# Three Strassen-like sets of projections in a hybrid decoder layer: the gates' set first, the group's attention behind the last set, and both halves of a weight's cast issued inside one job

## The chip, the cores and the metric

The kernel runs on one core of a Trainium2 chip. The metric is the device time of one execution in microseconds (us), lower is better. The kernel before was timed three times: 1045.32, 1046.86 and 1047.52 us, median 1046.86.

## What is computed

One layer of a decoder trunk on 512 tokens of width 1024, all in float32. `u` is the normed input. One wide projection gives queries, keys and values of three attention groups, the input of a pooling branch, the inputs of a state-space branch (`z`, `xbc`, `dt`) and three gates.

```python
u = rmsnorm(x, ln1_g[i])
proj = u @ w_in[i]
q, k, v, pool_in, z, xbc, dt_raw, gate_pre = jnp.split(proj, split_idx, axis=-1)
y_a = dilated_attention_mixer(q, k, v, rel_bias) @ w_a[i]
y_b = pool_mixer(pool_in, pool_w[i], pool_scale[i]) @ w_b[i]
y_c = ssd_mixer(z, xbc, dt_raw, ...) @ w_c[i]
gates = jax.nn.sigmoid(gate_pre + b_gate[i]).reshape(b, s, N_BRANCH, D_MODEL)
merged = gates[:, :, 0] * y_a + gates[:, :, 1] * y_b + gates[:, :, 2] * y_c
x = x + merged @ w_o[i]
x = x + conv_ffn(rmsnorm(x, ln2_g[i]), ...)
return rmsnorm(x, final_g)
```

## The kernel before

**Products.** A float32 product is made of three passes on TensorE (`mm3`, L234): weight and activation are each split into a rounded part and a remainder, and high x high, high x low and low x high are summed in PSUM. The activations `uh` and `ul` are split once. A weight is split for each job: a DMA brings `raw` (L183, SP's queue), ACT rounds it into `wh` (`cast`, L195), DVE subtracts to get `wl` (`low`, L215). `wh` has three buffers, `wl` and `raw` two.

**Jobs and their order.** `program()` yields the jobs in a list written by hand; between them stand `Call`s, which run other code at that place. Every engine works through its own instructions in the order in which this Python emits them. Ahead of job n, `prepare` emits `low` of job n+1, `cast` of job n+2 in two halves, and the DMA of job n+3. The two halves of a cast are not emitted at once: they wait in the list `second`. `flush()` emits what waits there, and the first half puts the second one into the list. `flush()` is called by every `step()` and, until the list is empty, ahead of each job. `step()` also takes the next item from `waiting` (attention heads, state-space chunks) and moves the running ones on by one stage, so these small pieces lie between jobs.

**The three sets.** Twelve blocks of 128 columns (queries and keys of attention group 1, and six of the eight blocks of gate 1; the other two are ordinary jobs) are computed in three sets. A set takes two blocks as its left side and two as its right side and replaces eight products of half size by seven, the jobs "one" to "seven": each 24 matmuls of 128x256 with sums of the activations (`sah`, `sbh`) and of the weights. The weights of "two" and "three" come by DMA as `raw`; the others are made in the set's tile `W`, by DVE (`plus`, L349) and by adding DMAs from POOL (L370). Behind its matmuls a job's `use` takes the PSUM bank: ACT copies it (L731), then the sinks of the blocks finish it. A query or key sink is one DVE or ACT operation (L678, L681, L689). A gate sink adds on DVE (L1221, L1229), takes the sigmoid on ACT (L1215) and multiplies into `MG` on DVE (the tile `yo`, L1218); in job "seven" it does this for one block after the other.

Before, the sets were: set 0 with queries and keys 0 and 1; set 1 with query and key 2 and gates 0 and 1; set 2 with gates 2 to 5. The sets overlap in a fixed list; written as (set, job), the last nine are (2, one), (1, seven), (2, five), (1, four), (2, three), (2, two), (2, six), (2, seven), (2, four), with a spare `xbc` job (a whole block, `pa`, 24 matmuls of 128x512) ahead of (2, seven) and of (2, four). The first nine are (0, one), (0, five), (0, two), (0, three), (0, six), (1, one), (0, seven), (1, five), (0, four). Behind (1, four) stood `attend(1)`, which puts six head items and the statistics of group 1 into `waiting`. An item: scores on TensorE (`ps`, L799), bias and maximum on DVE (L813, L817), four exponentials with sums on ACT (L820), transposes on TensorE (`pt`, L827), a copy, and for each pair the output product (`po`, L840). Behind the sets come `BC(0, 8)`, eight blocks of `xbc` in four jobs with ordinary `pa` chunks, then `ssd_start` (twelve Silu on ACT, L1144) and the queries and keys of group 2 (`pqk`).

## Time and profile before

| | us |
|---|---|
| median of three runs | 1046.86 |
| the profiled execution | 1044.88 |
| its span on the core | 1043.1 |
| TensorE (PE) busy | 1025.3 |
| DVE busy | 699.1 |
| ACT busy | 490.1 |

The profiled execution is 1.78 us longer than its span, and 1.98 us under the median. Rows of the timeline give start, duration, engine, line, operation with output and inputs, shape, and in brackets how long the engine stood idle ahead of it and what ended that. A row may merge several instructions (x4). Matmuls are pipelined, so starts are to be compared, not ends. PEclk is the clock granted to TensorE, 1.00 being full speed. The chain of waits is followed back from the last instruction.

### The profile page before, as it was taken

What the parts mean: (1) busy time and instruction counts of PE and PEld (TensorE: products, weight loads), DVE (VectorE), ACT (ScalarE), POOL (GpSimd) and SP (SyncE); (2) the same over time, 40 slices, a digit from 0 to 9 for tenths busy, and PEclk for the clock granted to TensorE, in tenths of its full rate; (3) what the DMA queues carried; (4) which work ended last, traced back from release to release, by engine and by line L of the source; (5) the groups of instructions that cost most, each with busy time, mean ns of one, the idle gap of its engine ahead of it and who ended that gap; (6) DMA issues with size and microseconds to landing.
All of it is one profiled execution on the core that took longest, in us unless ns stands there. A gap on an engine that the chain in (4) does not pass through costs nothing.

```text
span 1043.1 us, 13694 instructions
## 1 busy us (share of the span) xinstructions
PE 1025.3 (98%) x5420; PEld 870.1 (83%) x5420; DVE 699.1 (67%) x938; ACT 490.1 (47%) x815; POOL 161.7 (15%) x135
## 2 busy tenths in 40 slices
PE   9999999999988999999999999999999999999997
PEld 9998878899977878888888888898888888888885
DVE  5553566777757658767667755767677776766775
ACT  5432544445557454565565333545445344453342
POOL 1770000001100003310134500001110000111120
PEclk9999999999998999999999999999999999999999
DMA  8344312156532236453244535443223324323142
GB/s 285 116 128 137 116 46 74 33 135 147 119 104 91 82 101 162 94 155 77 81 132 140 178 100 210 165 143 112 91 81 122 119 73 172 121 81 122 61 141 81
DMA packets 121919, 123.16 MB, mean 118 GB/s; under 512 B 5603, under 2 KB 104230, under 8 KB 121855
## 3 DMA queue, kind: packets, MB, share of 16 engines
q1 hardware_dynamic: 118543, 119.07, 36.2%
q0 software_dynamic: 2720, 2.36, 1.7%
q8 instruction: 42, 0.69, 0.3%
q10 hardware_dynamic: 592, 0.86, 0.2%
q14 instruction: 22, 0.18, 0.1%
HBM read 118.48 MB, written 2.22 MB: 116 GB/s over the span
## 4 chain that ended last, share of the span: by engine, by line
PE 93%; ACT 3%; DVE 2%; DMA 1%; issue 0%; ACTq 0%; DVEq 0%
PE pa L234 31%; PE pu L234 22%; PE p L234 15%; PE pb L234 8%; PE pqk L234 6%; PE pa L1696 2%; PE pu L1481 1%; PE ppw L234 1%; PE ps L799 1%; PE po L840 1%; PE pt L827 1%; PE py L1125 1%; DVE wl L215 1%; ACT sb L820 1%; DMA xin<-in_x_dram 1%; ACT wh L195 1%
## 5 line engine op out<-in xcount | busy, mean ns | idle before, releaser
L215 DVE TENSOR_TENSOR wl<-raw,wh 128x2048 fp32r<-128x2048 f32 (+3 forms) x94 | 208.8, 2223 | 57.3 <-ACT wh L195 50.1
L195 ACT CAST wh<-raw 128x1024 fp32r<-128x1024 f32 (+3 forms) x186 | 180.8, 994 | 44.5 <-DVE raw L339 26.4
L1342 DVE SCALAR_TENSOR_TENSOR hc<-pu,fcol,hc 128x510 f32<-128x510 f32 x88 | 65.8, 748 | 61.1 <-ACT hc L1339 59.5
L234 PE MATMUL pa<-uh,wh 128*128 128x512 f32 x336 | 87.8, 404 | 3.5 <-ACT wh L195 3.5
L234 PE MATMUL pu<-uh,wl 128*128 128x512 f32 (+1 forms) x352 | 83.7, 380 | 0.0
L234 PE MATMUL pu<-uh,wh 128*128 128x512 f32 (+1 forms) x352 | 83.5, 379 | 0.0
L234 PE MATMUL pu<-ul,wh 128*128 128x512 f32 (+1 forms) x352 | 83.5, 379 | 0.0
L234 PE MATMUL pa<-uh,wl 128*128 128x512 f32 x336 | 83.1, 389 | 0.4 <-DVE wl L215 0.4
L234 PE MATMUL pa<-ul,wh 128*128 128x512 f32 x336 | 83.1, 389 | 0.0
L234 PEld LDWEIGHTS pa<-uh,wh 128*128 128x128 f32 x336 | 62.2, 191 | 16.9 <-ACT wh L195 4.1
L234 PEld LDWEIGHTS pu<-uh,wl 128*128 128x128 f32 x352 | 64.1, 188 | 12.8 <-DVE wl L215 0.3
L234 PEld LDWEIGHTS pu<-ul,wh 128*128 128x128 f32 x352 | 64.2, 188 | 12.5
L234 PEld LDWEIGHTS pa<-uh,wl 128*128 128x128 f32 x336 | 63.0, 188 | 13.8 <-DVE wl L215 0.8
L234 PEld LDWEIGHTS pu<-uh,wh 128*128 128x128 f32 x352 | 64.1, 188 | 12.4
L234 PEld LDWEIGHTS pa<-ul,wh 128*128 128x128 f32 x336 | 63.1, 188 | 13.3
L1347 POOL TENSOR_TENSOR hc<-hc 128x512 f32<-128x512 f32 x22 | 30.4, 1382 | 278.9 <-DVE hc L1342 243.9
L1339 ACT ACTIVATE hc<-pu,fcol,fcol 128x512 f32<-128x512 f32 x40 | 31.2, 780 | 81.2 <-PE pu L234 80.9
L215 DVE TENSOR_TENSOR wl<-w,wh 128x1024 fp32r<-128x1024 f32 (+2 forms) x25 | 38.5, 1541 | 10.6 <-ACT wh L195 10.6
L820 ACT ACTIVATE sb<-sb,both 128x128 f32<-128x128 f32 (+1 forms) x72 | 30.1, 419 | 27.7 <-DVE both L817 17.6
L370 POOL DMA_DIRECT2D w<-in_w_in_dram x10 | 12.3, 1230 | 194.4 <-DVE w L349 164.8
L195 ACT CAST wh<-w 128x512 fp32r<-128x512 f32 (+2 forms) x50 | 35.2, 746 | 15.0 <-DVE w L349 9.7
L1344 ACT ACTIVATE hc<-hc 128x512 f32<-128x512 f32 x22 | 13.9, 632 | 42.7 <-DVE hc L1342 42.7
(382 smaller groups left out, 1955.7 us busy)
## 6 DMA issues: line engine op xcount, KB each, us to landing
raw<-in_ffn_w_up_dram SPq DMA_DIRECT2D x22, 1024.0 KB
raw<-in_w_in_dram SPq DMA_DIRECT2D x21, 1024.0 KB
raw<-in_ffn_w_down_dram SPq DMA_DIRECT2D x11, 1024.0 KB
raw<-in_w_in_dram SPq DMA_DIRECT2D x20, 512.0 KB
raw<-in_w_o_dram SPq DMA_DIRECT2D x8, 1024.0 KB
raw<-in_w_b_dram SPq DMA_DIRECT2D x4, 1024.0 KB
al<-ad SPq DMA_DIRECT2D x16, 256.0 KB
w<-in_ffn_w_down_dram SPq DMA_DIRECT2D x4, 1024.0 KB
```

What stands on the lines that cost most here:

```text
L195: act.copy(job.high[:, :, o], job.raw[:, :, o])
L215: (eng or dve).tensor_tensor(l[:, :, o], job.raw[:, :, o], h[:, :, o].bitcast(F32), OP.subtract)
L234: pe.matmul(ps, l, r, start=first and n == 0, stop=last and n == total - 1, skip_group_check=again)
L370: pool.dma_start(W[1][:, k:k + 2, at:at + n], src[:, k:k + 2, :], accum_op=OP.add)
L799: pe.matmul(pss[i][:, o:o + w * P], q[r, n * P:(n + 1) * P], k[r, kb * P:(kb + w) * P], start=True, stop=True)
L820: act.activation(sb[:, off:off + w * P], sb[:, off:off + w * P], AF.Exp, bias=nm[:, n, h:h + 1], accum_out=ls[:, n, h:h + 1])
L827: pe.transpose(pt[:, o:o + P], sb[:, o:o + P], eye)
L1339: act.activation(t, ps, AF.Identity, bias=ff["c1"][:, ff["b"] + m:ff["b"] + m + 1], scale=fw(2, m))
L1342: dve.scalar_tensor_tensor(t[:, sh:], ps[:, :S - sh], fw(k, m), t[:, sh:], OP.mult, OP.add)
L1344: act.activation(t, t, AF.Silu)
L1347: pool.tensor_tensor(a, a, t, OP.mult)
L1696: pe.matmul(first[2 * n + j][:, lo:hi], a[:, k, j * P:(j + 1) * P], b[:, k, lo:hi], start=a is wh and b is uh and k == 0, stop=a is wl and ...
```

## The change

The set of the four gates comes first, then the set with queries and keys 0 and 1, then the mixed one. The banks stay with the place in the list ("a", "c", "a"). `attend(1)` moves from behind (1, four) to behind the last job of all three sets. In a set's job, `flush()` is called after each of the two column halves, so both halves of the cast of job n+2 are emitted within job n and ahead of what `use` emits.

```diff
                 mm3(cut(ps, c), lambda k: wh[:, k, cs], lambda k: wl[:, k, cs],
                     lambda k: parts[k][0], lambda k: parts[k][1], range(4),
                     fresh and c == 0, True, again=not fresh or c == 1)
+                flush()
             use(name, ps)
...
         loads, s = zip(
-            set_of_sevens((Q(0), Q(1)), (K(0), K(1)), "a", (0.125, 0.125)),
-            set_of_sevens((Q(2), G(0, True)), (K(2), G(1, False)), "c", (0.125, 1.0)),
-            set_of_sevens((G(2, True), G(3, True)), (G(4, False), G(5, False)), "a"))
+            set_of_sevens((G(2, True), G(3, True)), (G(4, False), G(5, False)), "a"),
+            set_of_sevens((Q(0), Q(1)), (K(0), K(1)), "c", (0.125, 0.125)),
+            set_of_sevens((Q(2), G(0, True)), (K(2), G(1, False)), "a", (0.125, 1.0)))
...
             yield s[i][n]
-            if (i, n) == (1, "four"):
-                yield Call(lambda: attend(1))
+        yield Call(lambda: attend(1))
         yield from BC(0, 8, 256)
```

In the changed kernel lines 769 to 1588 have numbers one higher than before; the others keep theirs.

**ACT, start of the first set.** `one` and `five` are the copies of PSUM behind the jobs of these names; `wh` is a cast, from `raw` or from the set's tile `w`. Before:

```order
L195 COPY wh<-w_2148 128x4x128 x2
L731 ACTIVATE one<-p 128x512
L195 COPY wh<-raw 128x4x128 x2
L731 ACTIVATE five<-p 128x512
L195 COPY wh<-raw 128x4x128 x2
L195 COPY wh<-w_2148 128x4x128 x2
```

and now:

```order
L195 COPY wh<-w_2148 128x4x128 x2
L195 COPY wh<-raw 128x4x128 x2
L731 ACTIVATE one<-p 128x512
L195 COPY wh<-raw 128x4x128 x2
L731 ACTIVATE five<-p 128x512
L195 COPY wh<-w_2148 128x4x128 x2
L1216 ACTIVATE gr<-gr,col 128x256 x2
```

Each cast moved ahead of the copy that stood before it; the sigmoids of the gates' set are new at this place.

**DVE, jobs seven and four of the first set.** `wl<-w_2148` is the remainder that job four needs. Before:

```order
L215 TENSOR_TENSOR wl<-w_2196,wh 128x1024
L689 TENSOR_TENSOR k_2412<-five,r_2482 128x4x64
L689 TENSOR_TENSOR k_2413<-five,r_2482 128x4x64
L215 TENSOR_TENSOR wl<-w_2148,wh 128x1024
L215 TENSOR_TENSOR wl<-raw,wh 128x1024
```

and now:

```order
L215 TENSOR_TENSOR wl<-w_2196,wh 128x1024
L1230 TENSOR_TENSOR gr<-five,r_2480 128x256
L1219 TENSOR_TENSOR yo<-yo,gr 128x512
L1230 TENSOR_TENSOR gr<-five,r_2480 128x256
L1219 TENSOR_TENSOR yo<-yo,gr 128x512
L215 TENSOR_TENSOR wl<-w_2148,wh 128x1024
L215 TENSOR_TENSOR wl<-raw,wh 128x1024
```

Two key operations gave way to two pairs of a gate's difference and its product; each product takes a sigmoid that ACT makes from the difference ahead of it.

**ACT, end of the sets.** `sb` are the exponentials of attention, `gr` sigmoids, `xcv` and `xs` the evacuations of `xbc` blocks, `wh<-w_2521` the cast for the last jobs of set 2. Before:

```order
L195 COPY wh<-w_2521 128x4x128 x2
L959 ACTIVATE xcv<-pa,col 128x512
L195 COPY wh<-raw 128x8x64
L820 ACTIVATE sb,both<-sb,both 128x128 x4
L195 COPY wh<-raw 128x8x64
L731 ACTIVATE r_2985<-p 128x512
L1215 ACT_TABLE_LOAD
L1215 ACTIVATE gr<-gr,col 128x512 x2
L195 COPY wh<-w_2521 128x4x128
L820 ACT_TABLE_LOAD
L820 ACTIVATE sb,both<-sb,both 128x128 x4
L195 COPY wh<-w_2521 128x4x128
```

and now:

```order
L195 COPY wh<-w_2521 128x4x128 x2
L731 ACTIVATE r_2966<-p 128x512
L1216 ACTIVATE gr<-gr,col 128x512
L960 ACTIVATE xcv<-pa,col 128x512
L195 COPY wh<-raw 128x8x128 x4
L681 ACTIVATE q_2858<-p 128x4x64
L1216 ACTIVATE gr<-p,col 128x256
L960 ACTIVATE xs<-pa,col 128x512
L195 COPY wh<-raw 128x8x128
L821 ACT_TABLE_LOAD
L821 ACTIVATE sb,both<-sb,both 128x128 x4
```

The exponentials no longer stand between the halves of the casts; ACT's table loads from the first spare job to the end of the sets fall away, and the first one comes with the first exponential, behind the first `xs`.

## The prediction

> **What bounds the kernel now.** I read the page first, for the engine that is never free.

> ```profile
> PE 1025.3 (98%) x5420; PEld 870.1 (83%) x5420; DVE 699.1 (67%) x938; ACT 490.1 (47%) x815; POOL 161.7 (15%) x135
> ```

> TensorE is busy nearly all the time, so a change that leaves its matmuls alone can win only where it waits or where its clock is lowered. Next the busy times by stage: the sets before attention starts, the rest of the sets in two pieces, and the `xbc` jobs behind them.

> ```profile
> 236.00:271.00 35.00, 35.00 (x291) 34.87 (x291) 24.81 (x26) 17.88 (x35) 7.27 (x6) 1.00 0.70 172
> 271.00:292.00 21.00, 20.20 (x168) 19.13 (x167) 16.45 (x19) 11.21 (x22) 2.43 (x2) 1.00 0.32 63
> 292.00:327.00 35.00, 28.46 (x157) 24.23 (x156) 19.52 (x27) 22.81 (x56) 0.00 (x0) 0.90 0.22 69
> 327.00:374.00 47.00, 47.00 (x262) 38.52 (x263) 31.39 (x35) 22.10 (x39) 0.00 (x0) 1.00 0.37 112
> ```

> The first column is the stretch and its length, the next PE's busy time; 1.00 or 0.90 is PEclk. Sets without attention lose nothing (35.00 of 35.00), `xbc` jobs with attention lose nothing (47.00 of 47.00), but sets with attention lose 0.80 and 6.54 us, and there the clock falls. Then TensorE's timeline of that stretch:

> ```profile
> 236.18 0.63 PE L234 MATMUL p<-uh,wh 128*128 128x256 f32 x4
> 270.96 0.64 PE L234 MATMUL p<-uh,wh 128*128 128x256 f32 x4
> 282.29 0.74 PE L234 MATMUL p<-uh,wl 128*128 128x256 f32 x4 [0.56 <-DVE wl L215]
> 295.65 2.11 PE L234 MATMUL pa<-uh,wh 128*128 128x512 f32 x8 [1.27 <-ACT wh L195]
> 308.12 2.12 PE L234 MATMUL pa<-uh,wh 128*128 128x512 f32 x8 [2.18 <-ACT wh L195]
> 317.97 1.22 PE L234 MATMUL p<-uh,wl 128*128 128x256 f32 x4 [2.70 <-DVE wl L215]
> 321.55 3.18 PE L234 MATMUL pa<-uh,wh 128*128 128x512 f32 x8
> 328.98 1.16 PE L799 MATMUL ps<-k,q 64*128 64x128 f32 x16
> ```

> Every wait is for a weight's cast or its remainder. ACT's timeline says why the casts come late:

> ```profile
> 292.15 1.28 ACT L820 ACT_TABLE_LOAD   x1
> 295.00 0.60 ACT L195 CAST wh<-raw 128x512 fp32r<-128x512 f32 x1
> 312.94 1.28 ACT L820 ACT_TABLE_LOAD   x1
> 316.05 0.60 ACT L195 CAST wh<-w 128x512 fp32r<-128x512 f32 x1
> ```

> At 292.15 ACT loads a table, makes four exponentials, and the second half of a cast follows at 295.00; the matmul that needs it starts at 295.65. The same again before 317.97: the second half of a cast runs at 316.05, its remainder follows, and TensorE has stood 2.70 us. The clock:

> ```profile
> 316.00:318.00 2.00, 0.03 (x1) 0.04 (x1) 1.31 (x2) 2.00 (x5) 0.00 (x0) 0.81 0.00 0
> 318.00:321.50 3.50, 3.50 (x16) 3.50 (x17) 3.35 (x5) 0.27 (x2) 0.00 (x0) 0.50 0.00 0
> ```

> It drops to a half inside the wait of 2.70 us and not in the one of 2.18.

> **Part 1: attention leaves the sets.** I count TensorE's work from the first set job at 236.18 to the second scores at 328.98, that is 92.8 us. Twelve jobs of a set take 270.96 - 236.18 = 34.78, so 2.90 each, and 21 take 60.9. For the rest, the chain of waits has undisturbed pieces:

> ```profile
> 329.05 1.09 PE ps L799 x16
> 336.21 0.44 PE pt L827 x4
> 336.65 5.45 PE pa L234 x24
> ```

> Three `pa` chunks (two spares and the first `xbc` block) are 16.4, two scores 2.2, two transposes 0.9. Together 80.4. The stretch loses 92.8 - 80.4 = 12.4 us. That is more than the idle time (7.34), since the half clock slows what runs (the last chunk takes 328.98 - 321.55 = 7.43 instead of 5.45) and a stream that restarts loses a little each time.

> After the change nothing of attention is emitted before the first `xbc` block, so the sets hold casts, copies and the sinks alone, and the early flush starts each cast about one job sooner. The matmuls of attention stay as many; they follow `xbc` blocks of 5.45 us, where the row 327 to 374 has the same mix at no loss. I take the whole 12.4 back. Lower bound of this term: 5, if waits return behind the sets and half the clock loss stays; upper bound 12.4. The table loads and casts that crowded ACT cost TensorE nothing beyond these waits.

> What attention may meet at its new place is one row of ACT:

> ```profile
> 331.88 1.05 ACT L195 CAST wh<-raw 128x1024 fp32r<-128x1024 f32 x1 [2.02 <-DMA raw<-in_w_in_dram]
> ```

> A cast waits 2.02 for its DMA with the exponentials queued behind it. TensorE did not wait, since the transposes come steps later and there are other chunks. Cost 0, with that cover gone 2.0.

> **Part 2: casts in one job.** The cast of job n+2 now stands ahead of the copy of job n on ACT. Before, in the same place:

> ```profile
> 239.31 0.60 ACT L731 ACTIVATE one<-p 128x512 f32<-128x512 f32 x1 [0.81 <-PE p L234]
> 239.80 1.13 ACT L195 CAST wh<-raw 128x512 fp32r<-128x512 f32 x2
> 246.23 2.19 ACT L195 CAST wh<-w 128x512 fp32r<-128x512 f32 x4 [2.48 <-DVE w L349]
> ```

> The copy waits for the job's end, and the cast, which needs nothing of that job, stands behind it; now it fills the 0.81 us. The cost is a cast whose source is late, such as the one at 246.23: it would hold the copy. There the job is (0, two), whose sinks begin on DVE and need no copy on ACT. In set 0 the remainders were already in time (35.00 busy), so I count 0 here: what the edit can win, the 0.80 us of 271 to 292, lies in part 1. Bounds 0 and +1.7 (a copy and two sinks put between one late cast and its remainder, priced below).

> **Part 3: the gates' set first.** Here I expect a new wait. Job (0, seven) of the gates' set finishes two gates one after the other on DVE, each waiting for ACT, and the remainder for (0, four) is queued behind. The same chain ran at the end of set 2, in ACT's and DVE's timelines:

> ```profile
> 307.97 0.59 ACT L731 ACTIVATE r<-p 128x512 f32<-128x512 f32 x1
> 309.24 0.42 DVE L1229 TENSOR_TENSOR gr<-five,r 128x256 f32<-128x256 f32 x1
> 309.87 0.72 ACT L1215 ACTIVATE gr<-gr,col 128x512 f32<-128x512 f32 x1
> 310.63 0.69 DVE L1218 TENSOR_TENSOR yo<-yo,gr 128x512 f32<-128x512 f32 x1 [0.97 <-ACT gr L1215]
> 311.69 0.72 ACT L1215 ACTIVATE gr<-gr,col 128x512 f32<-128x512 f32 x1 [1.09 <-DVE gr L1229]
> 312.45 0.69 DVE L1218 TENSOR_TENSOR yo<-yo,gr 128x512 f32<-128x512 f32 x1 [0.79 <-ACT gr L1215]
> ```

> From the first sigmoid to the end of the second product it took 312.45 + 0.69 - 309.87 = 3.27. There a spare job of 5.45 covered it; now job four of 2.90 follows after one job. Before, set 0 had key operations here and the remainder came at

> ```profile
> 258.48 1.22 DVE L215 TENSOR_TENSOR wl<-w,wh 128x1024 fp32r<-128x1024 f32 x1
> ```

> With 2.90 a job, seven ends at 236.18 + 7 x 2.90 = 256.5. Copy 0.6, difference 0.45, then 3.27: 260.8; the remainder ends 1.25 later, at 262.1. Job four starts at 259.4 and needs it after 8 of its 24 matmuls, at 260.3. TensorE waits 1.8. Bounds 0 (if the sigmoids catch up) and 3. Late next would be the remainder of (1, two): on DVE it stands behind the two products of (0, four). That job needs it 2.90 + 0.96 = 3.9 after four ends. One sigmoid of at most 0.72 (the other runs beside the first product), 1.4 of products and 1.2 of subtraction make 3.3, so it is in time by 0.6. In the mixed set, now last, seven and four have one gate each and the spare jobs around them.

> **Part 4: the tail.** The last `po` and the statistics move behind the first `pqk` chunk. Before, TensorE waited there for the Silu:

> ```profile
> 380.78 1.16 PE L1056 MATMUL pcb<-xcv 128*128 128x128 f32 x8 [0.99 <-ACT xcv L1144]
> 374.62 1.04 ACT L195 CAST wh<-raw 128x1024 fp32r<-128x1024 f32 x1
> 375.68 1.28 ACT L1144 ACT_TABLE_LOAD   x1
> 323.05 0.56 ACT L828 COPY sb<-pt 128x512 f32<-128x512 f32 x1
> ```

> Now a transpose, `po` and the statistics lie ahead of `pcb` on TensorE (an estimate of 0.4 each, by the transposes' 0.44), and one more copy of 0.56 ahead of the Silu on ACT. The wait shrinks from 0.99 by 1.2 - 0.56: -0.7, bounds 0 and -1.0.

> On SP's and POOL's queues the loads of the mixed set (two narrow transfers for one wide) go from the second place to the third. POOL's four adding DMAs took, from first to last issue,

> ```profile
> 252.93 1.21 POOL L370 DMA_DIRECT2D w<-in_w_in_dram  x1 [9.11 <-ACT wh L195]
> 265.72 1.21 POOL L370 DMA_DIRECT2D w<-in_w_in_dram  x1 [3.81 <-issue]
> 273.98 1.20 POOL L370 DMA_DIRECT2D w<-in_w_in_dram  x1 [7.05 <-DVE w L349]
> ```

> 12.8 us, some 4 apart, each waiting for the one before. Begun at 273.98, where the third set begins them, they end near 291 with 4 for the last. Job (2, seven) starts at 236.2 + 19 x 2.90 + 5.45 + 1.8 = 298.5. Cost 0; without the spare job ahead, the cast would come just in time.

> **Sum** against the profiled execution: 1044.88 - 12.4 + 0 + 1.8 - 0.7 = 1033.6. The median lies 1.98 above that execution, so I forecast 1035.5 for the median.

> **The rivals.** *The new wait cuts the clock.* For it: the clock fell within a wait of 2.70 us. Against: not within 2.18, and I expect 1.8. From somewhere between 2.18 and 2.70 it decides. Price: half speed for about 6.5 us as from 317.5 to 324, a loss near 3.2, and a longer wait by 0.6: 1035.5 + 3.8 = 1039.3. [...]

> *Attention's waits come back behind the sets*: the casts of two `xbc` jobs, the sigmoids and the first table load meet on ACT. For it: the 2.02 row. Against: 327 to 374 loses nothing. Price: half of part 1, 6 us: 1041.5.

> *Slower: casts hold the copies.* Any cast whose source comes after the job's end now delays copy, sinks and, behind these on DVE, its own remainder: 0.60 + 1.1 (two sinks as the two differences here, 0.42 to 0.69 each) = 1.7 us a job, against 0 before. It decides from about eight of the 21 jobs: 8 x 1.7 = 13.6 is more than the 12.4 won. With ten, 1035.5 + 17 = 1052.5. For it: the row with 2.48 shows that late sources exist, and the one with 2.02 that everything behind a held cast is held. Against: the casts from 239.80 on run without a wait but for that one, and an earlier cast makes the next remainder, and so the next sum on DVE, earlier too.

> *The waits only move* and nothing is won: 1046.9; against it stand the stretches without loss.

> **Chances.** Forecast 0.66, clock cut 0.14, waits behind the sets 0.09, nothing won 0.04, slower 0.07. Faster by over 0.2% (2.1 us, about what a measurement here can tell from no change) has the first three, 0.89. The range holds the forecast with its bounds and most of the next two: low 1032.0 (no new wait, 1.8 less, and the runs lie up to 1.5 under their median), high 1041.0.

> **What would show it.** Right: one wait of TensorE of about 1.8 for `wl` near 260, with two `yo` rows ahead of that `wl` on DVE, no other over 1 us and PEclk 1.00 from there to the first `pqk`; the first `ps` near 236.2 + 60.9 + 3 x 5.45 + 1.8 = 315, and the exponentials behind it; `pcb` waiting under 0.6. Wrong: copies of ACT held by casts that wait for `w` or DMA, a clock of 0.50 after the gates' set, or waits of TensorE in the four `xbc` jobs.

## The result, and the profile after

The changed kernel took **1033.79 us** in the median (1031.99 to 1035.22, four runs), beside 1046.84 for the kernel before: a ratio of 0.9876, with a 95% interval of 0.9857 to 0.9896. The forecast was 1035.5, the range 1032.0 to 1041.0. The profiled execution, at 1035.22, is the slowest of the four; its span is 1033.4. The medians here and below are over all runs of a kernel and the ratios over fast runs, which leaves out one slow run of 3632.47 us, in order_alone.

First the busy times on the page after, which answer to the page's line of before.

```profile
PE 1022.2 (99%) x5420; PEld 868.8 (84%) x5420; DVE 698.8 (68%) x938; ACT 485.1 (47%) x811; POOL 161.2 (16%) x135
```

The work is the same, 5420 matmuls. ScalarE has four instructions fewer (811 for 815), all of them table loads (28 for 32). Next the busy times by stage of the changed kernel, over the stretches that the prediction showed: the stretch and its length, then busy PE, PEld, DVE, ACT and POOL with their counts of instructions, then PEclk, the DMA share and GB/s.

```profile
236.00:271.00 35.00, 32.69 (x257) 32.18 (x256) 24.30 (x27) 19.72 (x37) 4.84 (x4) 0.95 0.64 157
271.00:292.00 21.00, 21.00 (x177) 21.00 (x177) 16.10 (x17) 10.65 (x21) 4.84 (x4) 1.00 0.41 77
292.00:327.00 35.00, 35.00 (x200) 30.23 (x200) 23.08 (x28) 18.00 (x31) 0.00 (x0) 1.00 0.43 135
327.00:374.00 47.00, 47.00 (x283) 38.63 (x282) 32.82 (x38) 29.79 (x72) 0.00 (x0) 1.00 0.32 93
```

The loss has changed its place. Before, TensorE was full in the first row and idle for 6.54 us in the third, with the clock at 0.90. Now it is full from 271 to 374, at clock 1.00, and the first row loses 2.31 us of idle time and some clock. The two largest lines of TensorE's waits in the changed kernel (what waited and for whom, the sum, how many, the longest; the second also stands in the kernel before), and pieces of its timeline with the waits and the later places that the forecast named:

```profile
PE p L234 <- DVE wl L215: 2.3, 2, 1.7
PE pa L1653 <- DVE relb L502: 1.1, 1, 1.1
```

```profile
240.31 0.74 PE L234 MATMUL p<-sah,wl 128*128 128x256 f32 x4 [0.57 <-DVE wl L215]
...
262.63 1.00 PE L234 MATMUL p<-uh,wl 128*128 128x256 f32 x4 [1.75 <-DVE wl L215]
...
317.18 1.16 PE L800 MATMUL ps<-k,q 64*128 64x128 f32 x16
...
371.27 1.06 PE L1057 MATMUL pcb<-xcv 128*128 128x128 f32 x8
```

The 1.75 us before 262.63 are the new wait that part 3 announced; 0.57 more stand in an earlier job of that set. All waits of TensorE for `wh` are gone, and `pcb` at 371.27 waits for nothing. VectorE's timeline shows what stands ahead of the remainder that TensorE waits for:

```profile
257.71 0.43 DVE L1230 TENSOR_TENSOR gr<-five,r 128x256 f32<-128x256 f32 x1 [1.76 <-ACT r L731]
258.93 0.69 DVE L1219 TENSOR_TENSOR yo<-yo,gr 128x512 f32<-128x512 f32 x1 [0.79 <-ACT gr L1216]
259.54 0.42 DVE L1230 TENSOR_TENSOR gr<-five,r 128x256 f32<-128x256 f32 x1
260.75 0.69 DVE L1219 TENSOR_TENSOR yo<-yo,gr 128x512 f32<-128x512 f32 x1 [0.79 <-ACT gr L1216]
261.36 1.22 DVE L215 TENSOR_TENSOR wl<-w,wh 128x1024 fp32r<-128x1024 f32 x1
```

Two products, each idle 0.79 us ahead of it for a sigmoid, then `wl`. That is the chain worked out in the prediction, and `wl` ends at 262.6, just as TensorE goes on.

### The profile page after: what moved, and what is told of

Read it like the earlier page. It is cut to its first block, busy times and chain, and to the rows that moved or that the text cites. A ratio compares the mean times of both kernels' runs of the same rounds, so it can differ in the third digit from the quotient of the medians.

```text
span 1033.4 us, 13679 instructions
## 1 busy us (share of the span) xinstructions
PE 1022.2 (99%) x5420; PEld 868.8 (84%) x5420; DVE 698.8 (68%) x938; ACT 485.1 (47%) x811; POOL 161.2 (16%) x135
## 3 DMA queue, kind: packets, MB, share of 16 engines
q0 software_dynamic: 2720, 2.36, 1.7%
## 4 chain that ended last, share of the span: by engine, by line
PE 95%; DVE 2%; ACT 1%; DMA 1%; issue 0%; SPq 0%; ACTq 0%; DVEq 0%
PE pa L234 32%; PE pu L234 22%; PE p L234 14%; PE pb L234 8%; PE pqk L234 6%; PE pa L1696 2%; PE ps L800 1%; PE pu L1482 1%; PE ppw L234 1%; PE pt L828 1%; PE po L841 1%; PE py L1126 1%; DVE wl L215 1%; PE pa L1653 1%; DMA w<-in_w_in_dram 1%; PE pyo L1133 1%
## 5 line engine op out<-in xcount | busy, mean ns | idle before, releaser
L215 DVE TENSOR_TENSOR wl<-raw,wh 128x2048 fp32r<-128x2048 f32 (+3 forms) x94 | 208.7, 2222 | 44.9 <-ACT wh L195 35.6
L195 ACT CAST wh<-raw 128x1024 fp32r<-128x1024 f32 (+3 forms) x186 | 180.5, 994 | 46.8 <-DVE raw L339 26.3
L1343 DVE SCALAR_TENSOR_TENSOR hc<-pu,fcol,hc 128x510 f32<-128x510 f32 x88 | 65.8, 748 | 60.9 <-ACT hc L1340 59.3
L234 PE MATMUL pa<-uh,wh 128*128 128x512 f32 x336 | 86.5, 399 | 0.0
L234 PE MATMUL pu<-uh,wl 128*128 128x512 f32 (+1 forms) x352 | 83.7, 380 | 0.0
L234 PE MATMUL pu<-uh,wh 128*128 128x512 f32 (+1 forms) x352 | 83.5, 379 | 0.0
L234 PE MATMUL pu<-ul,wh 128*128 128x512 f32 (+1 forms) x352 | 83.5, 379 | 0.0
L234 PE MATMUL pa<-ul,wh 128*128 128x512 f32 x336 | 83.0, 389 | 0.0
L234 PE MATMUL pa<-uh,wl 128*128 128x512 f32 x336 | 83.0, 389 | 0.0
L234 PEld LDWEIGHTS pu<-uh,wl 128*128 128x128 f32 x352 | 64.1, 188 | 12.8 <-DVE wl L215 0.3
L234 PEld LDWEIGHTS pu<-ul,wh 128*128 128x128 f32 x352 | 64.2, 188 | 12.5
L234 PEld LDWEIGHTS pu<-uh,wh 128*128 128x128 f32 x352 | 64.1, 188 | 12.4
L234 PEld LDWEIGHTS pa<-ul,wh 128*128 128x128 f32 x336 | 63.1, 188 | 13.3
L234 PEld LDWEIGHTS pa<-uh,wl 128*128 128x128 f32 x336 | 63.1, 188 | 13.1
L234 PEld LDWEIGHTS pa<-uh,wh 128*128 128x128 f32 x336 | 61.2, 188 | 12.8 <-issue 0.7
L195 ACT CAST wh<-w 128x512 fp32r<-128x512 f32 (+2 forms) x50 | 35.3, 748 | 21.6 <-DVE w L349 10.2
L370 POOL DMA_DIRECT2D w<-in_w_in_dram x10 | 12.3, 1229 | 203.8 <-DVE w L349 150.8
L215 DVE TENSOR_TENSOR wl<-w,wh 128x1024 fp32r<-128x1024 f32 (+2 forms) x25 | 38.4, 1540 | 8.1 <-ACT wh L195 5.9
```

Source lines behind the costliest of these rows:

```text
L195: act.copy(job.high[:, :, o], job.raw[:, :, o])
L215: (eng or dve).tensor_tensor(l[:, :, o], job.raw[:, :, o], h[:, :, o].bitcast(F32), OP.subtract)
L234: pe.matmul(ps, l, r, start=first and n == 0, stop=last and n == total - 1, skip_group_check=again)
L370: pool.dma_start(W[1][:, k:k + 2, at:at + n], src[:, k:k + 2, :], accum_op=OP.add)
L1343: dve.scalar_tensor_tensor(t[:, sh:], ps[:, :S - sh], fw(k, m), t[:, sh:], OP.mult, OP.add)
```

## The experiments

Each kernel was compared with runs of the kernel before on the same chip: their median was 1045.61 for the first four kernels, 1045.66 for the next four and 1045.64 for the last two.

**attend_alone: before, with only the attention moved.**

```diff
             yield s[i][n]
-            if (i, n) == (1, "four"):
-                yield Call(lambda: attend(1))
+        yield Call(lambda: attend(1))
```

> The kernel before, with only the attention of group 1 moved behind the last job of the three sets (old order of the sets, no early flush). Theory 1, attention inside the sets is what made casts late there: most of the gain comes, no wait of TensorE over 1 us between 283 and 330, PEclk 1.00 there, the waits of 270 to 283 (about 1.5 in all) stay; 1034 to 1037 us. Theory 2, the early flush makes the gain (casts were late because they stood behind copies): nothing, 1046 to 1048 us with waits over 2 us at the spare jobs.

Measured 1032.89, ratio 0.9879 [0.9865, 0.9892]: 12.7 us less, about as much as the whole change, and 1.1 below the range expected. The two largest lines of TensorE's waits and the busy times by stage:

```profile
PE pa L1652 <- DVE relb L502: 1.1, 1, 1.1
PE p L234 <- DVE wl L215: 0.8, 2, 0.6
```

```profile
236.00:271.00 35.00, 34.95 (x290) 34.61 (x288) 24.76 (x27) 18.46 (x37) 7.27 (x6) 1.00 0.71 169
271.00:292.00 21.00, 20.24 (x162) 19.59 (x163) 15.12 (x18) 10.89 (x23) 2.43 (x2) 1.00 0.39 77
292.00:327.00 35.00, 34.73 (x188) 29.12 (x188) 25.28 (x31) 19.49 (x37) 0.00 (x0) 1.00 0.39 120
```

The 6.54 us of the third stretch are down to 0.27, and the wait for `pcb` is gone here too, so it belongs to this move. What stays is the 0.76 us of the second stretch (about 1.5 was expected).

**order_alone: before, with only the gates' set put first.**

```diff
-            set_of_sevens((Q(0), Q(1)), (K(0), K(1)), "a", (0.125, 0.125)),
-            set_of_sevens((Q(2), G(0, True)), (K(2), G(1, False)), "c", (0.125, 1.0)),
-            set_of_sevens((G(2, True), G(3, True)), (G(4, False), G(5, False)), "a"))
+            set_of_sevens((G(2, True), G(3, True)), (G(4, False), G(5, False)), "a"),
+            set_of_sevens((Q(0), Q(1)), (K(0), K(1)), "c", (0.125, 0.125)),
+            set_of_sevens((Q(2), G(0, True)), (K(2), G(1, False)), "a", (0.125, 1.0)))
```

> The kernel before, with only the gates' set put first (attention still begins behind job four of the second set, no early flush). Theory 1: attention's waits at the spare jobs stay and the new wait at job four of the gates' set is added, 1.8 us or more and half clock behind it; 1048 to 1051 us. Rival, the sigmoids between the exponentials made the trouble and the new order takes them away: 1040 us or less.

Measured 1046.52, ratio 1.0008 [0.9999, 1.0016]. By stage:

```profile
236.00:271.00 35.00, 32.38 (x264) 31.56 (x263) 24.51 (x27) 19.34 (x37) 4.84 (x4) 1.00 0.65 156
271.00:292.00 21.00, 21.00 (x184) 20.87 (x182) 16.18 (x18) 9.29 (x19) 4.84 (x4) 1.00 0.41 77
292.00:327.00 35.00, 28.35 (x166) 24.05 (x165) 20.40 (x27) 23.52 (x56) 0.00 (x0) 0.95 0.25 75
327.00:374.00 47.00, 47.00 (x256) 38.20 (x255) 30.45 (x34) 21.54 (x38) 0.00 (x0) 0.96 0.37 111
```

The new waits came (2.62 us idle in the first stretch), but the 0.80 of the second stretch went; the net cost is below the time expected and too small to tell from none. With attention still in the sets, its stretch loses as much idle time as before (6.65). The clock loses as much as before too: 0.95 in the third stretch for 0.90, but 0.96 in the fourth for 1.00.

**flush_alone: before, with only the early cast.**

```diff
                     fresh and c == 0, True, again=not fresh or c == 1)
+                flush()
```

> The kernel before, with only the early flush in the sets' jobs (old order, attention still inside the sets). Theory 1: the waits before 283 go (1.5 us) and some of those at the last set's jobs, those at the spare jobs stay, since a spare job's cast is still cut by exponentials; 1041 to 1046 us. Theory 2: most of the gain, 1034 to 1037 us.

Measured 1043.82, ratio 0.9982 [0.9974, 0.9991]: 1.8 us won, a small gain that the forecast had put at nothing. The long waits stay, one of 3.9 among them:

```profile
PE pa L234 <- DVE wl L215: 3.9, 1, 3.9
PE p L234 <- DVE wl L215: 2.5, 2, 2.1
PE pa L234 <- ACT wh L195: 2.2, 1, 2.2
```

```profile
292.00:327.00 35.00, 26.88 (x149) 21.98 (x147) 19.93 (x26) 21.35 (x49) 0.00 (x0) 0.95 0.26 82
```

In this trace the gain is not one of shorter waits. The stretch idles 8.12 us for 6.54 before, and from 236 to 374 TensorE idles 8.59 us for 7.34. The clock stands at 0.95 for 0.90 in this stretch.

**no_flush: the changed kernel without that line.**

> The changed kernel without the early flush. Theory 1: a small loss; at job four of the gates' set the cast now also stands behind the second sigmoid, so the wait of 1.75 us grows to 2.3 to 3; 1034.5 to 1037 us. Theory 2: the gain is lost, 1045 us or more.

Measured 1034.59, ratio 0.9893 [0.988, 0.9905]. The waits in the gates' set are these:

```profile
PE p L234 <- ACT wh L195: 1.4, 1, 1.4
PE p L234 <- DVE wl L215: 1.1, 2, 0.6
```

At job four there are now two, 1.35 for the cast and 0.57 for its remainder, 1.92 in all where 2.3 to 3 was expected; the other 0.57 stands in an earlier job. Together they are 2.5, and 1.8 in after_again below. The early cast is thus probably worth something in the changed kernel as well, 0.0010 to 0.0017 of the time by the ratios 0.9883 and 0.9876 of its two comparisons; after_again ran on another chip, and the intervals overlap.

**after_again: the changed kernel once more, beside the next three.**

> The changed kernel once more, unchanged, beside the others of this group. Theory: the wait of about 1.75 us at job four of the gates' set is there in every run, and TensorE's clock is halved behind it only when most of that wait falls into one 3.413 us step of a fixed grid, so it may or may not be halved in this trace; 1032 to 1035 us. Rival, the halved clock follows from the length of the wait alone: halved again at the same place.

Measured 1033.41, ratio 0.9883 [0.987, 0.9897]. It shows the same wait, 1.8, without the half clock: PEclk is 1.00 in all four stretches from 236 to 374 (last section).

**old_order: the changed kernel with the sets in the order of before** (the diff of order_alone the other way round).

> The changed kernel with the old order of the sets (queries and keys first, gates last), attention behind all sets and early flush kept. Theory, the gates-first order only adds the wait at its job four: no wait of TensorE over 0.3 us in the sets, full clock, 1.5 to 3.4 us less than the changed kernel beside it, so 1030.5 to 1032 us where that one takes 1033.5. Rival, the order of the sets helps: not faster than the changed kernel.

Measured 1031.55, ratio 0.9863 [0.985, 0.9877], 1.86 under after_again beside it. The gates' set at the front costs time, as part 3 said. The remaining wait of TensorE there is 0.5, in the mixed set; that was expected under 0.3.

**late_product: the changed kernel, where a right-hand gate's product is emitted one step later.**

```diff
             if hi:
                 gate(t, t)
-                times()
+                def later():
+                    times()
+                    return
+                    yield
+                running.append(later())
```

> The changed kernel, but a right-hand gate's product into the merge tile is emitted one step later, behind the remainder for job four. Theory, the two product rows ahead of that remainder make the wait: the wait of 1.75 us goes, 1.5 to 3.4 us less than the changed kernel beside it. Rival, the copy and the sigmoids on ACT make it: the wait stays over 1 us.

Measured 1031.05, ratio 0.986 [0.9845, 0.9875], 2.36 under after_again. VectorE's timeline ahead of the same job four:

```profile
256.28 0.76 DVE L1230 TENSOR_TENSOR gr<-five,r 128x256 f32<-128x256 f32 x2 [2.23 <-ACT r L731]
256.96 1.22 DVE L215 TENSOR_TENSOR wl<-w,wh 128x1024 fp32r<-128x1024 f32 x1
258.10 1.29 DVE L1219 TENSOR_TENSOR yo<-yo,gr 128x512 f32<-128x512 f32 x2
```

The products now stand behind `wl`, and no wait for a weight is left in the sets. With this one change the order that cost 1.86 us costs nothing, and it has the lowest median of the study, half a microsecond under old_order.

**one_table: before, with Exp for Sigmoid in the gates' sinks**, which leaves out the gates' true values and four of the five table loads from the sets to the twelve Silu behind them.

> The kernel before with attention inside the sets, but the gate sinks take the exponential in place of the sigmoid (the gates' values are left out, the time of the operation is the same), so ACT loads one table instead of five from the sets to the Silu. Theory A, the loads of 1.28 us among the casts are a good part of attention's cost in the sets: 1038 to 1043 us. Theory B, the exponentials between the halves of the casts cost by their place alone: 1044 us or more, with the waits at the spare jobs near 2 us.

Measured 1044.71, ratio 0.9991 [0.9982, 1.0]: 0.9 us, with an interval from nothing to 1.9. The third stretch still loses 7.16:

```profile
292.00:327.00 35.00, 27.84 (x156) 23.58 (x155) 20.34 (x27) 19.02 (x52) 0.00 (x0) 0.94 0.21 65
```

So the table loads are not what starved TensorE in the main.

**late_exp: before, attention in the sets, each head's exponentials one step later.** This one came from a row of ScalarE's timeline of the kernel before, at the wait of 2.18 us:

```profile
305.91 0.40 ACT L820 ACTIVATE sb<-sb,both 128x128 f32<-128x128 f32 x1 [3.19 <-DVE both L817]
```

The exponential stands 3.19 us at the head of ScalarE's queue for its maximum, and the second half of the cast stands behind it and starts at 307.46.

```diff
+            if g == 1:
+                yield
             for n, kb, w, off in spans:
                 act.activation(sb[:, off:off + w * P], sb[:, off:off + w * P], AF.Exp,
...
             yield
-            yield
+            if g != 1:
+                yield
```

> The kernel before, attention still inside the sets, with one edit: in group 1 the four exponentials of a head are emitted one step later than the sum and the maximum on VectorE that feed them. In the kernel before, ScalarE stands about 3.2 us at the first exponential until the maximum comes, with a half of a weight's cast queued behind it. If it is this wait for input at the head of ScalarE's queue that starves TensorE, the exponentials now find their input ready, the casts pass, TensorE's waits of 2.18 and 2.70 us between 292 and 327 shrink to under 1 us each, the clock stays at 1.00 there, and 5 to 9 us are won: 1037 to 1041. If it is the busy time of the exponentials (1.7 us) and the table loads (1.3 us) that stand between the halves of a cast, nothing changes in these and the time stays within 2 us of before: 1044 to 1047.

Measured 1037.73, ratio 0.9924 [0.991, 0.9937]: 7.9 of the 12.7 us, with attention still in the sets, and table loads and exponentials still between the halves of two casts. ScalarE's rows where the exponentials now stand, the product that needs the cast, and the stage:

```profile
299.95 0.61 ACT L195 CAST wh<-raw 128x512 fp32r<-128x512 f32 x1
300.58 1.28 ACT L822 ACT_TABLE_LOAD   x1
301.88 0.40 ACT L822 ACTIVATE sb<-sb,both 128x128 f32<-128x128 f32 x1
...
303.43 0.60 ACT L195 CAST wh<-raw 128x512 fp32r<-128x512 f32 x1
```

```profile
304.09 2.14 PE L234 MATMUL pa<-uh,wh 128*128 128x512 f32 x8 [0.18 <-ACT wh L195]
```

```profile
292.00:327.00 35.00, 33.29 (x197) 27.25 (x197) 25.93 (x34) 25.47 (x52) 0.00 (x0) 1.00 0.38 117
```

The first exponential starts at the end of the load, its input ready; the stretch loses 1.71 instead of 6.54, and the clock stays at 1.00. A load and four exponentials still stand between the halves of this cast, and TensorE waits 0.18 for it; in the kernel before it waited 2.18, without a load there but with the exponential that stood 3.19 for its input. For this wait the cause is thus the exponential that waited, not the time that an exponential or a table load takes. Not all of the 7.9 is shown to be that: the wait of 1.27 stood behind a load and exponentials with no idle time between them, and went because the exponentials now come after that cast. How the later wait of 2.70 hangs on the others was not taken apart; it shrank along with them, to 0.5.

**old_late: the two repairs together.**

> The changed kernel with the sets in their old order (queries and keys first) and the right-hand gate's product emitted one step later. Each of the two alone took 1.9 and 2.4 us off the changed kernel by removing the same wait of 1.75 us before job four of the first set. If that wait is all that either removes, the two together give no more than one: 1030.5 to 1032, ratio to the kernel before 0.985 to 0.987. If the late product also frees VectorE's queue elsewhere (the wait of 0.47 us that the old order has near 280), it comes at 1030 to 1030.8.

Measured 1031.33, ratio 0.9863 [0.985, 0.9877]: no more than either alone, as expected if both remove the same wait. The 0.47 in the mixed set stayed.

## Why the prediction was right, step by step

Beside each term of the sum, what the runs gave for it:

| term | forecast, us | measured, us | from |
|---|---|---|---|
| 1 and 4: attention leaves the sets; the tail | -12.4 - 0.7 | -12.7 | attend_alone |
| 2: casts in one job | 0 | -1.8; -1.2; -1.3 | flush_alone; after_again less no_flush; old_order less attend_alone |
| 3: gates' set first | +1.8 | +1.9; +1.7 | after_again less old_order; no_flush less attend_alone |
| sum | -11.3 | -13.05; -12.25 | the two comparisons of the change |

The forecast of 1035.5 is 1033.6 + 1.98, which is 1035.6; nothing hangs on the difference.

**Part 1** was right in size, and the move alone gives it. Its cause was read half right. The prediction named the table load and the four exponentials between the halves of a cast. one_table shows that the loads count for about 1 us, at most 1.9, and late_exp that 7.9 of the 12.7 come back when the exponentials are emitted one step later. For the wait of 2.18 it was the exponential that waited for its maximum; the others were not separated. Had the rows of ScalarE been read with their idle time, the 3.19 would have been seen. In the new place such waits exist and are covered, as this row of the changed kernel shows:

```profile
328.53 0.40 ACT L821 ACTIVATE sb<-sb,both 128x128 f32<-128x128 f32 x1 [2.76 <-DVE both L818]
```

A cast there also waits 1.47 for its DMA, and yet TensorE is full between 271 and 374.

**Part 2** is the term that was mis-sized, forecast at nothing. Alone it is -1.8 with an interval that excludes nothing won; the other two values come from pairs on different chips whose intervals overlap. With these sizes the terms add up to -12.0 to -12.8, so this one can account for the difference between the forecast of -11.3 and the measured -12.25 to -13.05. The stretch taken as proof, set 0 at 35.00 of 35.00, only showed that there was nothing to win in that set. The 0.80 of 271 to 292, which the prediction took to be all that this edit can win, shrank only to 0.47 in flush_alone and went in order_alone, without the edit. How the early cast wins its time stays open in part: with attention moved, TensorE's waits in the sets fall from 2.5 to 1.8 in one pair and from 0.8 to 0.5 in the other, and alone it wins although they grow.

**Part 3** came as worked out: one wait, at job four of the gates' set, for `wl` behind two `yo` rows, 1.75 us for 1.8. late_product shows that these products are the cause. That the time agrees as closely, +1.9 for +1.8, is in part luck: old_order has a wait of 0.47 of its own, so the order adds about 1.3 of waiting, and the rest fits a half clock in some of the runs, which the sum did not hold. Not foreseen were the 0.57 at 240.31, which after_again doesn't have: there the remainder stands behind a cast, the cast behind the sum `w`, and that one waits 0.61 for a DMA. The first scores at 317.18 stand 2.2 later than the 315 of the forecast: the 0.57 and the half clock (3.41 us at half speed, about 1.7) make 2.3, less 0.4 because the first set began that much earlier.

**Part 4**: the 0.99 ahead of `pcb` went to nothing, so -1.0 at its bound for -0.7.

**The rivals.** The first, that the new wait cuts the clock, was rated 0.14 and came true in the profiled execution, with the clock of 0.50 behind the gates' set that was named as a sign of being wrong, but at half its price, since one step of half clock followed and not two. It was probably no accident of that execution, although a trace shows it only there: of the eight runs of the changed kernel, the four with a granted clock of 0.996 or 0.997 took 1033.91 to 1035.22 us and the four at 0.998 or 0.999 took 1031.99 to 1033.32. The means are 1.7 apart, as much as one step of 3.41 at half speed costs. The deciding point of this rival, between 2.18 and 2.70 us of wait, was wrong (last section). The waits behind the sets did not come back. No cast held a copy so as to make TensorE wait between 271 and 327. "Nothing won" is excluded by the result, whose interval ends at 0.9896.

## What to carry to other kernels

Here an exponential that waited 3.19 us for its input at the head of ScalarE's queue held the cast queued behind it, so look at the idle time ahead of an instruction before its duration: emitting the exponentials one step later gave back 7.9 us, putting them where jobs are 5.45 instead of 2.90 us long gave 12.7. When jobs are put in another order, write down what then stands ahead of each late operand on its engine; the rows of the order gave the new wait to within 0.1 us, and moving one product behind the remainder took it away again. A term put at nothing because one stretch was full has to be checked in the stretches that were not.

## What the runs showed of the hardware

```profile
259.51:262.92 3.41, 1.67 (x14) 1.46 (x13) 2.62 (x5) 2.93 (x6) 0.00 (x0) 1.00 0.43 66
262.92:266.34 3.42, 3.42 (x18) 3.42 (x18) 1.92 (x2) 0.46 (x2) 0.00 (x0) 0.50 0.76 209
266.34:269.75 3.41, 3.41 (x31) 3.41 (x30) 2.90 (x4) 2.72 (x6) 0.00 (x0) 1.00 0.85 252
```

Busy 1.67 of 3.41, then a whole step at 0.50 with 18 matmul records for the usual 31. In after_again no fall marks the grid near the wait, which lasts from 259.97 to 261.72; only an estimate places it. The mean clock of 0.999 over 1031.1 us leaves 1.0 to 3.1 us of half clock. If these stand at the end of the span, as in the two traces above, 225 steps counted back from there give an edge between 260.0 and 262.1. With the edge at 261.08:

```profile
257.67:261.08 3.41, 2.30 (x20) 2.10 (x18) 2.27 (x4) 2.31 (x5) 0.00 (x0) 1.00 0.59 77
261.08:264.49 3.41, 2.77 (x23) 2.77 (x24) 2.91 (x4) 1.83 (x5) 0.00 (x0) 1.00 0.47 129
264.49:267.91 3.42, 3.42 (x31) 3.42 (x30) 3.42 (x4) 2.46 (x5) 0.00 (x0) 1.00 1.09 316
```

By this estimate the grid split the wait: the steps are idle for 1.11 and 0.64 us, neither for half. The clock stays at 1.00. The kernel before fits, and there the falls themselves give the grid: its wait of 2.18 fell across two steps, idle for 1.07 and 1.11 us, with the clock at 1.00 behind them, and of the one of 2.70 1.99 us lay in one step.

```profile
303.60:307.01 3.41, 2.34 (x26) 1.84 (x24) 2.21 (x4) 1.10 (x6) 0.00 (x0) 1.00 0.00 0
307.01:310.42 3.41, 2.30 (x10) 1.91 (x11) 1.56 (x2) 3.38 (x8) 0.00 (x0) 1.00 0.02 6
...
313.84:317.25 3.41, 1.42 (x13) 1.21 (x11) 1.78 (x3) 3.14 (x12) 0.00 (x0) 1.00 0.00 1
317.25:320.66 3.41, 2.69 (x12) 2.69 (x13) 3.34 (x5) 1.02 (x2) 0.00 (x0) 0.50 0.00 0
320.66:324.08 3.42, 3.42 (x12) 2.87 (x11) 0.77 (x2) 2.59 (x10) 0.00 (x0) 0.50 0.00 0
```

How much idle time in a step it takes was not shown. In the middle of the kernels 1.74 us in one step had a fall behind it (the changed kernel, from 259.51), and 1.27 us had none (the kernel before, from 293.36). Where TensorE's work ends, steps idle for 1.37 us (the changed kernel, from 1024.09) and 1.71 us (the kernel before, from 1034.05) had none. In flush_alone the rows show half speed behind the wait of 3.89 us, where eight matmuls took 3.65 us and eight ahead of it 1.97, and none behind those of 2.18 and 2.06, where eight took 2.11 and four 0.74. Two things don't fit so simply: in the kernel before, a second step at 0.50 follows one with only 0.72 us idle, and in after_again, by the estimate above, a step idle for 1.86 us, where TensorE's work ends at 1023.80 and the edge is at 1025.66, had no fall behind it. No kernel was built to move a wait along the grid.
